# A two-block transformer kernel on one core: the gated delta-rule scan by column halves with both directions in one output product, and the second block's convolution, index choice and attention in another arrangement of PSUM banks

## The chip, the cores and the metric

The kernel runs on one core of a Trainium2 chip. The core has TensorE (PE in the rows; PEld is its weight load), VectorE (DVE), ScalarE (ACT), GpSimd (POOL) and SyncE (SP, which issues most DMAs). Each engine takes its instructions in the order in which they stand in its own queue, and semaphores hold an instruction until what it reads is written and what it overwrites is free. The metric is the device time of one execution in microseconds (us); a time is the median of several runs.

## What is computed

A model in two blocks, all in fp32, for 256 tokens ("lat") and 256 context tokens ("ctx") of 1024 features. The first block has two layers; the mixer of its layer 0 is a gated delta-rule network (GDN) scanned in both directions, beside a latent attention (MLA). The second block has two layers, each with a mixer (sparse attention, a causal convolution with 31 taps, a pooling) and a feed-forward part.

```python
# GDN: one step of the scan, for each of 8 heads, chunks of 64 tokens, state s of 64x64
v_new = u_i - einsum('bhck,bhkv->bhcv', w_i, s)
o_i = einsum('bhck,bhkv->bhcv', qd_i, s) + einsum('bhcs,bhsv->bhcv', qk_i, v_new)
s = s * gl_i[..., None, None] + einsum('bhck,bhcv->bhkv', kd_i, v_new)
# run over ctx, then lat, forwards, and over both flipped, backwards; the two outputs are added

# second block, mixer of a layer; u = rmsnorm(h) @ w_in, cut into q, k, v, qi, ki, wi, u_conv, u_pool
idx = einsum('bths,bth->bts', relu(einsum('bthd,bsd->bths', qi, ki)), wi) * idx_scale   # 16 index heads
_, sel = lax.top_k(where(causal, idx, -inf), 64)       # for each token the 64 keys that it may attend
y_attn = softmax over the chosen keys (q k) @ v        # 8 heads of 64, 2 kv heads, query blocks of 128
y_conv = silu(layernorm(conv31(a * sigmoid(g)) + conv_b)) @ conv_pw     # 256 channels
y_pool = windowed means @ pool_w * pool_scale
mix = concatenate([y_attn, y_conv, y_pool]) @ w_out
```

## The kernel before, in words

A projection in fp32 is made of three matmuls on split operands (`mm3`, L554 to L556: high by high, low by high, high by low); weights come by DMA into `wraw`, ACT casts them to `whi` (L270) and DVE or POOL makes the low half `wlo` (L272). Plain fp32 matmuls stand in the rows with two PE instructions each, transposes with one. PSUM has eight banks of 128x512 fp32, handed out by kind from `Banks`; a bank of a kind is taken again only when the readers of its last content are done. The order of the instructions in each engine's queue is made while the program is built: a planner in the framework takes the instructions of the program text and interleaves them wherever their operands and buffers allow it by its own estimate of durations. So work written one after the other (the scan, then MLA) runs interleaved, and what stands in the rows is the planner's order.

**The scan (layer 0).** The kinds are `g` 3 banks, `s` 2, `tp`, `po` and `gv` one each; `aux` is `g` and `acc` is `s`. `gdn_run` (L1216) goes over four blocks i of 128 tokens and, in each, first over direction 0 and then over direction 1 (which walks the blocks in the order 1, 0, 3, 2 and the halves of a block backwards). `gdn_operands` makes a block's operands: `pu` (L1158) and two `pw` (L1160, L1163), three banks of `g`, which ACT copies to `gu` (L1165) and `gwq` (L1168, L1169). `gdn_state` then takes the two halves `a` of 64 tokens: `ps` = w and q times the state (L1192, four 128x128 matmuls), `gvn` = u minus `ps` (DVE, L1195), `pS` = kd^T times gvn (L1199: for each of four head pairs a 64x128 by 64x128 product into 128 partitions, of which only the two 64x64 blocks on the diagonal are used), the state S times its decay (POOL, L1206) plus `pS` (DVE, L1207), and `po` = Q times gvn (L1210, eight 64x64 products, all with the same half of the rows). `gdn_o` (L1175) adds the outputs. Around that, while the scan waits, PE runs `mod_chunk` (L373, the modulation vectors) and `l0_mla` (L787): four pairs of heads with two scores and two softmaxes each in `attend` (L665: scores, L676 maximum, L678 exp, L681 transposes into the scores' own bank, L683 copy, L689 value products into `po`). The first two pairs use the two `s` banks for scores, the late ones one `s` and one `g`; the tags `p` and `pt` have K.np = 2 buffers. `gdn_post` and `gdn_out` (L1252) end the layer's mixer.

**The mixer of the second block**, run twice (`s_mixer`, L1677). The kinds are `acc` 2 banks, `aux` 1, `s` 2, `tp` 2, `po` 1. The program's text is: `choose(1)` and later `choose(0)` (index scores of query block 1 or 0 into `s`, relu on ACT L1614 into `irl`, weighting on DVE L1621, then `s_topk`: eight rounds of MAX8 and MATCH_REPLACE8 on DVE, L1636 and L1637, and the mask L1639), the projections, `qkv`, `conv` (L1540: for each of two channel halves c and 32 taps, of which the last is the bias, a product for each of two token blocks; one block in `po`, one in `tp`), `pool_out`, `finish` (batch statistics L1551, reciprocal root in small DVE steps, `lnx` L1556 which reads the convolution's banks, transposes L1559 into an `acc` bank, then L1562, L1565 and the products L1569), and `att(1)`, `att(0)`. `s_attend` is called for each of two groups and makes two units hh: scores with the mask (L1654 and mm3) into `s`, maximum L1657, exp L1662, transposes L1664 into `tp`, a copy L1665, value products L1669 into the single `po` bank, scaling L1673. `out_features` transposes the result (L728, L306). The products with `w_out` follow. The weight pool `K.px` of the projections is closed after the mixer (L2037).

## Time and profile before

| | before |
|---|---|
| median of 3 runs | 2125.01 us (2121.82 to 2138.47) |
| the profiled execution, its own time | 2124.6 us |
| its span in the profile | 2122.8 us |
| PE busy | 1991.6 us, 94% of the span |
| DVE, ACT, POOL busy | 62%, 44%, 11% |
| mean granted TensorE clock | 0.957 of full speed |

A row of a stretch gives the busy time of each engine with its number of instructions, the granted clock of TensorE (1.00 is 2.4 GHz, 0.50 is 1.2 GHz) and what the DMAs moved. In a row of the timeline several equal instructions that follow one another are put together (x8), and what stands in brackets is how long the engine sat idle before it, and for whom.

### The profile page before, as it was taken

How to read it: one execution, taken by the hardware profiler on the slowest of the kernel's cores; microseconds unless marked ns; L12 is line 12 of the kernel's file. 1: busy time of each engine (PE TensorE's matmuls, PEld its weight loads, DVE VectorE, ACT ScalarE, POOL GpSimd, SP SyncE). 2: the span in 40 equal slices, each digit the busy share in tenths (PEclk: the TensorE clock that was granted, in tenths of full speed). 3: DMA queues.
4: the chain of work that ended last, by engine and by line, in shares of the span. 5: the costliest groups of instructions: out<-in, count | busy, mean ns of one | idle time of the engine just before them, and what ended most of it. 6: DMA issues, size and time to landing. Idle time of an engine off the chain costs nothing.

```text
span 2122.8 us, 31144 instructions
## 1 busy us (share of the span) xinstructions
PE 1991.6 (94%) x11656; PEld 1626.7 (77%) x11656; DVE 1315.5 (62%) x2729; ACT 924.7 (44%) x1620; POOL 242.1 (11%) x312
## 2 busy tenths in 40 slices
PE   6989799889999999979898999998999999989998
PEld 3868468768888778868666888897788789868886
DVE  5557457766777754454786555575765558576644
ACT  4533443354222233343565443564554445555532
POOL 2120212301000000020401001110200021020000
PEclk8999789899999999989898999998999999999999
DMA  8344542132568542213235664522656535055551
GB/s 284 90 120 101 179 130 66 46 109 80 179 213 279 164 158 90 89 53 120 70 99 159 184 194 137 155 87 62 197 179 190 180 97 147 21 169 184 188 188 66
DMA packets 186951, 291.88 MB, mean 137 GB/s; under 512 B 28472, under 2 KB 75704, under 8 KB 186800
## 3 DMA queue, kind: packets, MB, share of 16 engines
q1 hardware_dynamic: 172720, 272.54, 41.2%
q0 software_dynamic: 5472, 16.13, 2.4%
q10 hardware_dynamic: 8608, 1.23, 0.5%
q8 instruction: 91, 1.49, 0.3%
q14 instruction: 60, 0.49, 0.1%
HBM read 281.44 MB, written 8.41 MB: 137 GB/s over the span
## 4 chain that ended last, share of the span: by engine, by line
PE 85%; DVE 5%; DMA 4%; ACT 3%; issue 2%; POOL 1%; SPq 0%; ACTq 0%; DVEq 0%; POOLq 0%
PE acc L554 19%; PE acc L556 19%; PE acc L555 19%; PE s L554 3%; PE s L555 2%; PE s L556 2%; PE po L689 2%; PE tp L890 2%; PE po L1540 1%; PE tp L1540 1%; DMA wraw<-in_w_mod_dram 1%; PE gv L373 1%; PE aux L728 1%; PE aux L489 1%; PE g L1199 1%
## 5 line engine op out<-in xcount | busy, mean ns | idle before, releaser
L272 DVE TENSOR_TENSOR wlo<-wraw,whi 128x512 fp32r<-128x512 f32 (+4 forms) x772 | 483.4, 670 | 299.1 <-ACT whi L270 283.3
L270 ACT CAST whi<-wraw 128x1024 fp32r<-128x1024 f32 (+4 forms) x420 | 413.5, 990 | 496.4 <-PE acc L556 192.9
L554 PE MATMUL acc<-whi,u 128*128 128x512 f32 (+3 forms) x1320 | 508.5, 388 | 15.4 <-ACT u L306 9.6
L556 PE MATMUL acc<-whi,u 128*128 128x512 f32 (+3 forms) x1320 | 505.2, 384 | 1.7 <-DVE u L307 1.7
L555 PE MATMUL acc<-wlo,u 128*128 128x512 f32 (+3 forms) x1320 | 506.0, 385 | 0.2 <-DVE wlo L272 0.2
L554 PEld LDWEIGHTS acc<-whi,u 128*128 128x128 f32 x1320 | 251.3, 191 | 66.0 <-ACT u L306 11.6
L556 PEld LDWEIGHTS acc<-whi,u 128*128 128x128 f32 x1320 | 251.0, 190 | 50.4 <-DVE u L307 3.8
L555 PEld LDWEIGHTS acc<-wlo,u 128*128 128x128 f32 x1320 | 251.4, 191 | 47.4 <-DVE wlo L272 1.4
L554 PE MATMUL acc<-u,whi 128*128 128x512 f32 (+1 forms) x480 | 171.0, 362 | 1.8 <-ACT u L306 1.7
L555 PE MATMUL acc<-u,whi 128*128 128x512 f32 (+1 forms) x480 | 171.0, 358 | 0.2 <-DVE u L307 0.2
L556 PE MATMUL acc<-u,wlo 128*128 128x512 f32 (+1 forms) x480 | 171.1, 360 | 0.0
L272 POOL TENSOR_TENSOR wlo<-wraw,whi 128x512 fp32r<-128x512 f32 (+1 forms) x68 | 84.7, 1276 | 409.7 <-ACT whi L270 409.7
L432 DVE SCALAR_TENSOR_TENSOR msum<-mraw,u,msum 128x512 f32<-128x512 f32 x140 | 100.8, 747 | 15.2 <-DMA mraw<-in_w_mod_dram 14.1
L554 PEld LDWEIGHTS acc<-u,whi 128*128 128x128 f32 x480 | 91.0, 191 | 17.4 <-issue 2.6
L555 PEld LDWEIGHTS acc<-u,whi 128*128 128x128 f32 x480 | 91.9, 192 | 15.0 <-issue 1.7
L556 PEld LDWEIGHTS acc<-u,wlo 128*128 128x128 f32 x480 | 91.5, 191 | 15.0 <-issue 1.7
L307 DVE TENSOR_TENSOR u<-aux,u 128x512 fp32r<-128x512 f32 (+2 forms) x96 | 59.5, 632 | 41.0 <-ACT u L306 40.8
L554 PE MATMUL acc<-whi,dxh 128*128 128x512 f32 x176 | 69.7, 396 | 1.9 <-ACT dxh L306 1.9
L306 ACT CAST u<-aux 128x512 fp32r<-128x512 f32 (+2 forms) x96 | 50.6, 543 | 47.6 <-PE aux L728 34.9
L555 PE MATMUL acc<-wlo,dxh 128*128 128x512 f32 x176 | 69.6, 396 | 0.0
L556 PE MATMUL acc<-whi,dxl 128*128 128x512 f32 x176 | 69.0, 396 | 0.0
L307 DVE TENSOR_TENSOR dxl<-u,dxh 128x1024 fp32r<-128x1024 f32 x22 | 26.7, 1225 | 52.5 <-ACT dxh L306 52.5
(521 smaller groups left out, 3089.6 us busy)
## 6 DMA issues: line engine op xcount, KB each, us to landing
wraw<-in_w_up_dram SPq DMA_DIRECT2D x64, 512.0 KB, 4.0
wraw<-in_w_down_dram SPq DMA_DIRECT2D x64, 512.0 KB, 4.0
mraw<-in_w_mod_dram SPq DMA_DIRECT2D x56, 512.0 KB, 4.7
wraw<-in_w_ffn_down_dram SPq DMA_DIRECT2D x44, 512.0 KB, 3.8
wraw<-in_w_mod_dram SPq DMA_DIRECT2D x40, 512.0 KB, 5.9
wraw<-in_w_ffn_gate_dram SPq DMA_DIRECT2D x48, 256.0 KB, 3.1
wraw<-in_w_ffn_up_dram SPq DMA_DIRECT2D x48, 256.0 KB, 3.6
wraw<-in_w_ffn_gate_dram SPq DMA_DIRECT2D x20, 512.0 KB, 4.5
```

The costliest lines, as they stand in the source:

```text
L270: self.K.nc.scalar.copy(hi, raw)
L272: e.tensor_tensor(lo[:, k], raw[:, k], hi.bitcast(F32)[:, k], op=ALU.subtract)
L306: (hi_eng or nc.scalar.copy)(hi, src)
L307: nc.vector.tensor_tensor(lo, src, hi.bitcast(F32), op=ALU.subtract)
L373: nc.tensor.matmul(ps[32 * j:32 * j + 32, :], K.cl[:, g + k, :], raw[:, k, :], start=(g + k < 4), stop=(g + k >= 4))
L432: nc.vector.scalar_tensor_tensor(accs[s], raw[:, k, :], c, accs[s], op0=ALU.mult, op1=ALU.add)
L554: mm(ps, ah, bh, start=start, stop=False)
L555: mm(ps, ah, bl, start=False, stop=False)
L556: mm(ps, al, bh, start=False, stop=stop)
L689: nc.tensor.matmul(po[hh * 64:hh * 64 + 64, c:c + 128], v(hh, j), pts[hh][0][:, j * 128:(j + 1) * 128], start=(j == 0), stop=(j == nj - 1))
L890: nc.tensor.matmul(tp[:, t * 128:(t + 1) * 128], x[:, t // 2, t % 2 * 128 + j:t % 2 * 128 + j + 128], dg[j], start=(j == 0), stop=(j == 4))
L1540: nc.tensor.matmul(ps[t][:, c * 128:c * 128 + 128], yp[:, c, t * 128 + j:t * 128 + j + 128] if j < 31 else ones, dg, start=(j == 0), stop= ...
```

## The change

In the scan, `gdn_state` makes `pS` of 64x64 products, eight in the place of four of 64x128, which alternate between the two column halves hh and write only what is used; it uses half a bank. The product `po` is taken out of it: `gdn_run` makes the operands of both directions first, then for each of the two steps of a block the state of direction 0 and of direction 1, and then one `po` bank for both, with the products of the two directions alternating (direction 0 and 1 use different halves of the rows and of the partitions). In MLA the units of the first two pairs rotate over `s`, `s`, `tp`, those of the late ones over `s`, `s`, `tp`, `g`, `g`, `g`, with three `p` and `pt` buffers.

In the second block the convolution has one bank for both token blocks; the bias is one 512-wide product at its beginning (from four scaled identities in `irl` buffers) in the place of the 32nd tap. `att(1)` is written ahead of `conv` and `choose(0)`, in a pool of its own, for which the weight pool of the projections is closed inside the mixer. A unit of attention uses one bank for scores and transposes (`s` for hh = 0, `tp` for hh = 1), four `p` and `pt` buffers, and its value products go to `acc`; the transposes of `finish` go to `aux`.

```diff
@@ l0_mla
+    used = [0]
+    def unit(kinds):
+        used[0] += 2
+        return [kinds[(used[0] + i) % len(kinds)] for i in range(2)]
+    K.np = 3
...
-                   ("s", "g") if late else ("s", "s"))
+                   unit(("s", "s", "tp", "g", "g", "g") if late else ("s", "s", "tp")))
@@ gdn_state
-    pS, po = aux(K), aux(K)
+        gdn_o(K, t, a, slice(64 - 64 * a, 128 - 64 * a), ps)
+    pS = aux(K)[:, :256].rearrange("p (q c) -> p q c", q=4)
     for p in range(4):
-        c = slice(p * 128, (p + 1) * 128)
-        nc.tensor.matmul(pS[:, c], kd[r, c], vn[r, c], start=True, stop=True)
+        for hh in range(2):
+            c = slice(p * 128 + hh * 64, p * 128 + hh * 64 + 64)
+            nc.tensor.matmul(pS[hh * 64:hh * 64 + 64, p, :], kd[r, c], vn[r, c], start=True, stop=True)
...
-    for h in range(8):
-        hs = slice(h * 64, h * 64 + 64)
-        nc.tensor.matmul(po[o, hs], Q[r, h, :], vn[r, hs], start=True, stop=True)
@@ gdn_run
-        for d in range(2):
-            t = i if d == 0 else (1, 0, 3, 2)[i]
-            ops = gdn_operands(K, d, t)
-            for a in ((0, 1) if d == 0 else (1, 0)):
-                gdn_state(K, d, i == 0 and a == d, t, a, *ops, K.S[d])
+        ts = [i, (1, 0, 3, 2)[i]]
+        ops = [gdn_operands(K, d, ts[d]) for d in range(2)]
+        for s in range(2):
+            vns = []
+            for d in range(2):
+                u, wq, kd, Q = ops[d]
+                a = s ^ d
+                vns.append((64 * a, Q, gdn_state(K, d, i == 0 and s == 0, ts[d], a, u, wq, kd, K.S[d])))
+            po = aux(K)
+            for h in range(8):
+                hs = slice(h * 64, h * 64 + 64)
+                for a, Q, vn in vns:
+                    K.nc.tensor.matmul(po[64 - a:128 - a, hs], Q[a:a + 64, h, :], vn[a:a + 64, hs], start=True, stop=True)
@@ s_conv
-        ps = [bank(K, "po"), bank(K, "tp")]
+        ps = bank(K, "po")
+        bias = cut(K, [128, 2, 256], F32, "irl", 3)
...
+        nc.tensor.matmul(ps, ones, bias.rearrange("p t f -> p (t f)"), start=True, stop=False)
...
-        back = acc(K)
+        back = aux(K)
@@ s_attend
-        ps = bank(K, "s")
+        ps = bank(K, ("s", "tp")[hh])
...
-        p, pt = cut(K, [128, 512], F32, "p", 2), cut(K, [128, 512], F32, "pt", 2)
-        tp = bank(K, "tp")
+        p, pt = cut(K, [128, 512], F32, "p", 4), cut(K, [128, 512], F32, "pt", 4)
+        tp = ps
...
-        po = bank(K, "po")
+        po = acc(K)
@@ s_mixer
-        cv = conv()
-        choose(0)
-        pool_out(0)
-        pool_out(1)
-        finish(cv)
-        att(1)
-        att(0)
+        closed(K, K.px)
+        W.drop()
+        with Pool(K, "at"):
+            att(1)
+            with On(K, pix):
+                cv = conv()
+                choose(0)
+                pool_out(0)
+                pool_out(1)
+                finish(cv)
+            att(0)
```

What the planner makes of it shows in the queues. The first place is PE's queue in the scan, one block after its start. Before, it reads as follows (`gwq`, `gkd`, `gQ` are the operands, `gu` and `gvn` the values u and v_new, `gv` is a modulation vector, `s` a bank of MLA):

```order
L1192 MATMUL g_2378<-u_129,gwq_2354 128x128 x4
L373 MATMUL gv_3299<-wraw_3300,u_124 32x512 x2
L373 MATMUL gv_3299<-wraw_3304,u_124 32x512 x2
L819 MATMUL s_3535<-const_id_75,u_3388 128x128 x4
L819 MATMUL s_3542<-const_id_75,u_3388 128x128 x4
L1199 MATMUL g_2385<-gvn_2383,gkd_2309 128x128 x4
L1210 MATMUL g_2386<-gvn_2383,gQ_2359 64x64 x8
```

In the changed program the same engine has at this place (L1200, L1209 and L1237 are the lines of w and q, of `pS` and of `po` now):

```order
L1209 MATMUL g_2464<-gvn_2461,gkd_2309 64x64 x8
L1200 MATMUL g_2477<-u_130,gwq_2408 128x128 x4
L373 MATMUL gv_3355<-wraw_3364,u_124 32x512 x2
L554 MATMUL s_3614<-whik_3608,u_3438 128x512
L555 MATMUL s_3614<-wlok_3609,u_3438 128x512
L556 MATMUL s_3614<-whik_3608,u_3439 128x512
L373 MATMUL gv_3355<-wraw_3368,u_124 32x512 x2
L1209 MATMUL g_2485<-gvn_2482,gkd_2363 64x64 x8
L1237 MATMUL g_2498<-gvn_2461,gQ_2359 64x64
L1237 MATMUL g_2498<-gvn_2482,gQ_2413 64x64
```

`pS` stands as eight small products, other work stands between the steps of the two directions, and `po` of both directions stands behind both states, the two taking turns. All 16 products of `po` in a step read this way. The scan's last product is row 1080 of PE's queue before and row 1190 now, and the work of MLA's later pairs stands behind it in both.

The second place is PE's queue at the end of the second block's first mixer. Before, behind the last product of the convolution and the scores of query block 0:

```order
L1559 MATMUL acc_12895<-const_id_75,lnx_12917 128x128 x2
L1669 MATMUL po_12967<-u_11625,pt_12958 128x64 x4
L1559 MATMUL acc_12895<-const_id_75,lnx_12921 128x128 x2
L1664 MATMUL tp_13049<-const_id_75,p_13047 128x128 x4
L1669 MATMUL po_12997<-u_11625,pt_12988 128x64 x4
L1664 MATMUL tp_13086<-const_id_75,p_13084 128x128 x2
L1569 MATMUL aux_12935<-u_12894,u_11638 128x256
```

Now the queue has there, with L1582 and L1592 as the lines of `finish` and L1677 as that of the mask (`u_11684`):

```order
L556 MATMUL s_13030<-u_12033,u_12105 128x128
L554 MATMUL s_13030<-u_12033,u_12111 128x128
L555 MATMUL s_13030<-u_12034,u_12111 128x128
L556 MATMUL s_13030<-u_12033,u_12112 128x128
L1582 MATMUL aux_13077<-const_id_75,lnx_13099 128x128 x2
L1582 MATMUL aux_13077<-const_id_75,lnx_13103 128x128 x2
L1592 MATMUL aux_13117<-u_13076,u_11694 128x256 x2
L1677 LDWEIGHTS u_11652
L1677 MATMUL s_13127<-u_11684,u_11652 128x128
```

The value products of query block 1 have moved ahead of the convolution's end. The last index scores of `choose(0)` (`s_13030`) have moved from the middle of the convolution to behind its last product, and all eight score products of query block 0 stand behind them and behind `finish`; between these two places PE has nothing else.

The third place is DVE's queue there. Before, the choice of query block 0 begins amid the convolution (`ply` belongs to the pooling, `u_11626` holds the index values):

```order
L1523 TENSOR_SCALAR ply_12883<-aux_12880,u_73 128x256
L1621 SCALAR_TENSOR_TENSOR u_11626<-irl_12855,u_11979,u_11626 128x128
L1621 SCALAR_TENSOR_TENSOR ipart_12770<-irl_12855,u_11979,ipart_12770 128x128
L307 TENSOR_TENSOR u_11602<-ply_12883,u_11601 128x256
L1622 TENSOR_TENSOR u_11626<-u_11626,ipart_12770 128x128
L1633 TENSOR_TENSOR u_11626<-u_11626,const_rest_11594 128x128
L1636 MAX m_12861<-u_11626 128x8
L1637 MATCH_REPLACE u_11626<-m_12861,u_11626 128x128
```

Now it begins among the small steps of the reciprocal root for the convolution's layer norm (`rsv`, `rsy`, `rst`), behind the convolution's end:

```order
L1645 TENSOR_TENSOR u_11682<-u_11682,ipart_12952 128x128
L327 SCALAR_TENSOR_TENSOR rsy_13087<-rst_13088,rsy_13087 128x2
L1656 TENSOR_TENSOR u_11682<-u_11682,const_rest_11650 128x128
L325 TENSOR_TENSOR rst_13088<-rsy_13087 128x2
L1659 MAX m_13043<-u_11682 128x8
L326 TENSOR_TENSOR rst_13088<-rst_13088,rsv_13085 128x2
L1660 MATCH_REPLACE u_11682<-m_13043,u_11682 128x128
```

Behind these rows the eight rounds go on, with `lnx`, `cz` and the end of `finish` among them, up to the mask (L1662), which the scores of query block 0 read.

## Rows read from the trace of the kernel before

**Rows 1.** The page's busy times: engine, busy us, share of the span, instructions.

```profile
PE 1991.6 (94%) x11656; PEld 1626.7 (77%) x11656; DVE 1315.5 (62%) x2729; ACT 924.7 (44%) x1620; POOL 242.1 (11%) x312
```

**Rows 2.** Stretches of the scan and mixers: busy time of each engine, clock, DMA.

```profile
core 0: us, PE busy (x) PEld busy (x) DVE busy (x) ACT busy (x) POOL busy (x), PEclk, DMA share, GB/s
266.00:320.00 54.00, 51.73 (x607) 38.39 (x607) 29.33 (x67) 23.42 (x46) 6.38 (x10) 0.90 0.42 130
355.00:425.00 70.00, 62.36 (x575) 51.61 (x573) 49.50 (x100) 22.20 (x57) 21.62 (x30) 0.83 0.13 39
1340.00:1453.00 113.00, 112.81 (x820) 104.70 (x818) 74.03 (x203) 65.10 (x157) 9.91 (x12) 1.00 0.36 101
1453.00:1474.00 21.00, 15.04 (x89) 12.97 (x89) 11.66 (x40) 7.23 (x23) 1.14 (x2) 0.78 0.04 15
1845.00:1870.00 25.00, 18.85 (x116) 15.98 (x114) 13.08 (x44) 7.33 (x23) 1.14 (x2) 0.82 0.04 13
```

**Rows 3.** Two 5 us stretches amid the second row above, the same columns.

```profile
400.00:405.00 5.00, 5.00 (x32) 4.66 (x30) 4.56 (x17) 0.00 (x0) 0.00 (x0) 0.50 0.00 0
415.00:420.00 5.00, 3.17 (x19) 2.39 (x18) 4.93 (x14) 2.13 (x6) 2.81 (x4) 1.00 0.28 89
```

**Rows 4.** Timeline of PE in the scan: start, duration, line, tile, count.

```profile
302.25 0.98 PE L1158 MATMUL g<-u,u 64*64 64x64 f32 x27
304.15 0.97 PE L1160 MATMUL g<-u,gke 64*64 64x64 f32 x32
330.12 1.16 PE L1199 MATMUL g<-gvn,gkd 64*128 64x128 f32 x8
331.20 1.14 PE L1210 MATMUL g<-gvn,gQ 64*64 64x64 f32 x16
348.68 1.09 PE L689 MATMUL po<-pt,u 128*64 128x128 f32 x14
```

**Rows 5.** Timeline near the scan's end: copies of operands, and a wait of PE.

```profile
395.89 0.59 ACT L1165 COPY gu<-g 128x512 f32<-128x512 f32 x1 [5.01 <-PE g L1158]
397.17 0.41 ACT L1169 COPY gwq<-g 128x256 f32<-128x256 f32 x1
399.69 1.79 PE L1199 MATMUL g<-gvn,gkd 64*128 64x128 f32 x8 [1.18 <-DVE gvn L1195]
```

**Rows 6.** Timeline of PE at the end of the second block's first mixer.

```profile
1448.77 0.39 PE L1540 MATMUL po<-dg,u 128*128 128x128 f32 x2
1452.54 0.27 PE L556 MATMUL s<-u,u 64*128 64x128 f32 x1
1456.17 0.69 PE L1559 MATMUL acc<-const_id,lnx 128*128 128x128 f32 x2 [3.35 <-DVE lnx L1556]
1459.53 1.81 PE L1669 MATMUL po<-u,pt 128*128 128x64 f32 x8
1463.78 1.00 PE L1669 MATMUL po<-u,pt 128*128 128x64 f32 x8
1470.59 0.66 PE L1669 MATMUL po<-u,pt 128*128 128x64 f32 x4 [0.16 <-DVE u L1673]
1473.87 0.80 PE L554 MATMUL acc<-whi,u 128*128 128x512 f32 x1 [1.62 <-ACT whi L270]
```

**Rows 7.** Timeline of that mixer: index choice, scores, maximum and exp of block 0.

```profile
1427.34 0.29 DVE L1633 TENSOR_TENSOR u<-u,const_rest 128x128 f32<-128x128 f32 x1
1436.79 0.29 DVE L1639 TENSOR_TENSOR u<-u,const_rest 128x128 bf16<-128x128 f32 x1
1445.17 0.22 PE L1654 MATMUL s<-u,u 128*128 128x128 bf16 x1
1445.80 0.23 PE L1654 MATMUL s<-u,u 128*128 128x128 bf16 x1
1450.59 0.42 DVE L1657 TENSOR_REDUCE anx<-s 128x2 f32<-128x256 f32 x1 [3.55 <-PE s L556]
1447.06 0.37 ACT L1662 ACTIVATE p<-s,anx 128x128 f32<-128x128 f32 x1 [0.53 <-DVE rs L1672]
```

More of the change, by code (lines that the diff above doesn't have):

```diff
@@ L1180, in gdn_o, with gdn_state @@
         K.nc.scalar.copy(K.O[o, t, :], ps[o])
-def gdn_state(K, d, first, t, a, u, wq, kd, Q, S):
+def gdn_state(K, d, first, t, a, u, wq, kd, S):
     nc = K.nc
     r = slice(64 * a, 64 * a + 64)
-    o = slice(64 - 64 * a, 128 - 64 * a)
     if first:
@@ L1218, in gdn_run @@
     for i in range(4):
-        for d in range(2):
-            t = i if d == 0 else (1, 0, 3, 2)[i]
-            ops = gdn_operands(K, d, t)
-            for a in ((0, 1) if d == 0 else (1, 0)):
-                gdn_state(K, d, i == 0 and a == d, t, a, *ops, K.S[d])
+        ts = [i, (1, 0, 3, 2)[i]]
[11 more added lines that the diff above has]
+                    K.nc.tensor.matmul(po[64 - a:128 - a, hs], Q[a:a + 64, h, :], vn[a:a + 64, hs], start=True, stop=True)
+            for d in range(2):
+                a = s ^ d
+                gdn_o(K, ts[d], a, slice(64 - 64 * a, 128 - 64 * a), po)
 def gdn_post(K):
@@ L1526, in taps @@
     def taps(c):
-        for j in range(32):
+        for j in range(31):
             if j % 3 == 0:
                 dg = cut(K, [128, 3, 128], F32, "dg", 2)
-            nc.scalar.mul(dg[:, j % 3, :], K.ident, dw[:, i, c, j:j + 1] if j < 31 else dwb[:, i, c:c + 1])
+            nc.scalar.mul(dg[:, j % 3, :], K.ident, dw[:, i, c, j:j + 1])
             yield j, dg[:, j % 3, :]
     def conv():
-        ps = [bank(K, "po"), bank(K, "tp")]
+        ps = bank(K, "po")
+        bias = cut(K, [128, 2, 256], F32, "irl", 3)
+        for t in range(2):
+            for c in range(2):
+                nc.scalar.mul(bias[:, t, c * 128:c * 128 + 128], K.ident, dwb[:, i, c:c + 1])
+        nc.tensor.matmul(ps, ones, bias.rearrange("p t f -> p (t f)"), start=True, stop=False)
         for c in range(2):
@@ L1539, in conv @@
                 for t in range(2):
-                    nc.tensor.matmul(ps[t][:, c * 128:c * 128 + 128],
-                                     yp[:, c, t * 128 + j:t * 128 + j + 128] if j < 31 else ones, dg,
-                                     start=(j == 0), stop=(j == 31))
-        return ps
+                    nc.tensor.matmul(ps[:, t * 256 + c * 128:t * 256 + c * 128 + 128],
+                                     yp[:, c, t * 128 + j:t * 128 + j + 128], dg,
+                                     start=False, stop=(c == 1 and j == 30 and t == 1))
+        return [ps[:, t * 256:t * 256 + 256] for t in range(2)]
     def finish(ps):
         y = cut(K, [128, 2, 256])
-        back = acc(K)
+        back = aux(K)
         mv = cut(K, [128, 2, 2], F32, "bmv", 1)
@@ L1714, in qkv @@
             pairs_T(K, U[:, t, 0:512], 4, qh, ql, tk, 0.125)
-    with Pool(K, "ix"):
+    with Pool(K, "ix") as pix:
         choose = s_index(K, U, idx, mask)
```

12 lines of the change are left out of this document (4 added, 8 removed).

## The prediction, made before the changed kernel had run

> **What bounds the kernel now.** I read the page's busy times first: PE is busy for 94% of the span [rows 1], so a gain must take work from PE, fill one of the few stretches in which it waits or runs at the lower clock, or lengthen none. Then the table of stretches [rows 2]. Work at full clock is busy time times granted clock. From 355 to 425 us, the end of the scan with MLA beside it, 62.36 us of busy time at 0.83 are 51.8 us of work in 70 us: 18.2 us are lost. From 266 to 320 us it is 46.6 of 54 us, 7.4 lost. The second block's mixer is full until its convolution ends (112.81 of 113 us at 1.00), and then has a tail: 1453 to 1474 us holds 15.04 busy us at 0.78, 11.7 us of work in 21. The second run of the mixer has the same tail (18.85 busy of 25 us at 0.82). The two stretches of 5 us [rows 3] show the two forms of loss in the scan: all busy at 0.50 (2.5 us lost), or 3.17 busy at 1.00 (1.8 lost). At 399.69 PE waits 1.18 us for `gvn` with nothing else in its queue [rows 5]. Whatever the change does elsewhere, these two places decide.
>
> **The scan's products.** `po`: before, 16 steps of 16 instructions, 1.14 us each [rows 4], all in one quadrant of the array. A pair of directions takes 2.28 us, about 2.1 as the second overlaps the first one's end. Now the 32 instructions of a pair alternate between two quadrants that share neither rows nor columns. The nearest rows are L1158, 27 such instructions in 0.98 us, alternating so into one bank, and L1160, 32 in 0.97 us into two. I take 1.05 us; saved 1.05, in 8 pairs 8.4 us.
>
> The trace so far says that two row halves may write one bank at full pace: L1158 does [rows 4]. The Trainium skill's page "TensorEngine Tiling (Array Packing)", section Restrictions and Gotchas, says that different row tiles cannot access the same PSUM bank simultaneously; by that rule the pair would take turns and save nothing, and the sum below would come out 8.4 us higher. Here the row decides; the case is a rival below.
>
> `pS`: before, 8 instructions, and the next line starts 1.08 us later (330.12 to 331.20) [rows 4]. Now 16 of half the columns, alternating between column halves over the same rows. L689 alternates column halves with 128 columns: 14 instructions in 1.09 us, 0.06 apart, where L1199's are 0.13 apart. With 64 columns and the same overlap they would be 0.03 apart: 0.5 us. Without overlap the pace is that of L1210's 64x64, 0.06 apart: 1.0 us. I take 0.55 as L1158 has the same shape and 0.03; saved 0.53, in 16 steps 8.5 us (bounds 1.3 and 9.3). Together PE's work falls by 17 us; from 1 us if no halves overlap.
>
> **The scan's waits.** Products of MLA and of the modulation now stand between the two directions' steps, and the scan ends at a row of PE's queue with MLA's first pairs still unfinished, so the waits for `gvn` are covered to the end. MLA's late pairs then run on six banks instead of two. Of the 18.2 us lost I give back 12; the rest stays, because a softmax's chain of maximum, exp, transposes and copy still has to run for the last units. Bounds 5 and 18. On the other side, operands of direction 1 stand directly behind those of direction 0 and need the same three `g` banks, which ACT copies out one after the other, 395.89 to 397.58, 1.7 us [rows 5]. In four blocks that is 7 us at most, 0 where other products cover; I take 4. `gQ` is loaded for both directions at once, but is read only in the last product of a step; later loads on SP's queue don't stand behind a wait that is longer than before. Scan: -17 - 12 + 4 = -25 us.
>
> **The second block's tail.** Edits that I cost at nothing: the convolution has 124 products and one four times as wide instead of 128, each 0.39 us or less [rows 6]; ACT makes 66 scaled identities instead of 64, ahead of PE as now. Both lie in the full stretch; uncovered, the bias would cost its own product and two of the four extra identities, under 3 us. The earlier closing of the weight pool lets nothing start sooner that PE waits for: the first product with `w_out` waits for ACT's cast behind the last split of the attention [rows 6], and still does.
>
> What moves is dearer. Ahead of the convolution's end come four value products of block 1, 1.00 us each [rows 6], and eight transposes for them, by the 0.69 us of two at half clock about 1.4 us: +5.4. Behind it go six units of scores of block 0, 0.63 us each (1445.17 to 1445.80) [rows 7]: -3.8. So the last index scores end at about 1452.8 + 1.6 = 1454.4 us (1452.8 is the end of the last score before the wait, rows 6). Then the choice of block 0, which lay under the convolution, is exposed, because its eight rounds on DVE start only now and the scores of block 0 wait for its mask. Before, it took from 1427.34 to 1437.08, 9.7 us, with seven foreign instructions in between [rows 7]. Now some sixteen foreign ones stand between, small ones mostly, for which I add 1.0, and 1.2 for the relu and the weighting of the last unit ahead of it: 11.9 us in which PE has only `finish`, about 1.5 us of work. Then eight units of scores. PE came back to full clock some 6 us after it resumed at 1456.17: eight instructions of L1669 took 1.81 us at 1459.53 and 1.00 at 1463.78 [rows 6]. The units are 5.0 us of work, and 6 us at half clock lose 3: 8.1. Behind the last score come maximum (0.42), two exps (0.37 each and their sums) [rows 7], transposes and a copy, together 2.2, and from the last value products to `w_out` 1470.59 to 1473.87 [rows 6], 3.3. So `w_out` would start at 1454.4 + 11.9 + 8.1 + 5.5 = 1479.9 us instead of 1473.87: 6.0 later, in two mixers +12 us. Bounds for one mixer: -1, if the choice needs 8 us and the clock stays, and +9, if the foreign instructions hold each round up.
>
> **Sum.** 2124.6 us for the profiled execution (its span is 2122.8, the rest lies around it), -25 and +12: 2111.6. The median of the runs is 0.4 us higher than that execution, so I say 2112.
>
> **Rivals.** *A, the forecast:* own range 2102 to 2122, chance 0.52.
>
> *B, the scan becomes dense and the tail costs little:* -17 and all of the 18.2 us, tail +2 in all: 2092. It speaks for it that MLA's rest now lies behind the scan with six banks; against it that the last units of MLA have nothing behind them and that PE's clock follows each gap. Chance 0.22. Half-way cases give 2094 to 2103.
>
> *C, the change doesn't do what it says in the scan:* the products get shorter, but the steps are bound by the way over DVE and POOL, so shorter products only make the waits longer, as the 1.18 us wait at 399.69 suggests [rows 5]. Then the gain is 9 us and the tail takes 12: 2128. Against it: before 355 us PE hardly waits. Chance 0.11.
>
> *D, the other side:* operands. If each of four double blocks stops PE for 4 us (two rounds of copies with no product that can pass) and half clock follows for 6 us (3 us), 28 us are lost; with -17 and +12 that is 2148. It decides from 5 us in each block on, where the kernel gets slower at all with nothing recovered. Against it: the queue has other products around three of the four blocks. Chance 0.10.
>
> *E, row halves wait for each other in `po`'s bank:* 8.4 us of the saving go: 2120. Chance 0.05, as L1158's pace [rows 4] speaks against it. This is the rule of the skill's page that stands above.
>
> **How the numbers follow.** About 1%, 21 us, is what a measurement of this kernel can tell from no change: faster is below 2104, slower above 2146. Faster: B and the lower end of A, 0.27. Slower: most of D and a little of C, 0.10. Between: 0.63. The range goes from B's middle, 2096, to just above C, 2131; outside lie D with 0.10 and the lower half of B with 0.10.
>
> **What would show it.** Right, if the products of `po` stand in the new profile as 32 in about 1 us and 16 of `pS` in about 0.5; if the scan's last stretch shows little idle time for `gvn`; and if in both mixers of the second block PE idles some 10 us between the last index scores and the mask, at half clock behind it, with `w_out` about 6 us later than the convolution's end would have it now. Wrong, if PE waits for ACT's copies at the operands (D), if 16 of `pS` still take 1 us, or if the rounds of the choice run ahead of the convolution's end.

## The result, and the profile of the changed kernel

The changed kernel takes 2105.9 us (median of 4 runs, 2103.1 to 2107.4) where the kernel before took 2123.9 beside it. The ratio is 0.9899 with a 95% interval of 0.9854 to 0.9945: by the ratio 21 us less, with an interval of 12 to 31; the two medians lie 18 us apart. Forecast were 2112 us, in a range of 2096 to 2131, and most of the chance within 1%; the ratio lies on that line. The direction is right and the gain of 13 us was taken some 5 to 8 us too small. The profiled execution of the changed kernel took 2107.4 us, the longest of the four; its span is 2105.6 us. One execution of a later run, of 9858 us with MLA's banks alone, counts in no time and no ratio below.

The page of the changed kernel, its span and the busy times:

```profile
span 2105.6 us, 31388 instructions
PE 1966.8 (93%) x11772; PEld 1603.0 (76%) x11772; DVE 1309.4 (62%) x2729; ACT 927.2 (44%) x1626; POOL 241.8 (11%) x312
```

PE has 25 us less busy time than before [rows 1] and the span is 17 us shorter. The table of stretches shows the two places that decided: the scan (two rows, the same stretches as in [rows 2]) and the tail of the second block's first mixer (three rows; the mixer lies 33 us earlier now).

```profile
core 0: us, PE busy (x) PEld busy (x) DVE busy (x) ACT busy (x) POOL busy (x), PEclk, DMA share, GB/s
266.00:320.00 54.00, 49.70 (x763) 36.42 (x758) 37.21 (x77) 24.62 (x55) 11.83 (x16) 1.00 0.48 151
355.00:425.00 70.00, 61.24 (x515) 46.46 (x513) 62.67 (x125) 34.98 (x86) 17.64 (x26) 0.97 0.18 61
1420.00:1424.00 4.00, 0.62 (x3) 0.46 (x4) 3.98 (x23) 0.00 (x0) 0.00 (x0) 0.60 0.56 173
1424.00:1429.00 5.00, 2.57 (x7) 1.30 (x6) 4.75 (x21) 1.22 (x3) 0.00 (x0) 0.50 0.21 76
1433.00:1440.00 7.00, 7.00 (x24) 4.95 (x23) 1.61 (x5) 2.34 (x10) 0.00 (x0) 0.50 0.00 0
```

In the scan the clock is 1.00 from 266 to 320 us where it was 0.90, and 0.97 from 355 to 425 where it was 0.83 [rows 2]. The second pair of rows doesn't hold the same work: the last product of `po` starts at 373.2 us now and started at 410.1 before. In the tail PE is busy for 0.62 of 4 us and then, from 1433 to 1440, for all of 7 us at 0.50. The timeline of PE in the scan (start, duration, line, tile, count) shows the new products:

```profile
330.53 0.68 PE L1209 MATMUL g<-gvn,gkd 64*64 64x64 f32 x16
331.14 1.16 PE L1200 MATMUL g<-u,gwq 128*128 128x128 f32 x8
335.31 1.09 PE L1237 MATMUL g<-gvn,gQ 64*64 64x64 f32 x29
336.34 1.16 PE L1200 MATMUL g<-u,gwq 128*128 128x128 f32 x8
```

Sixteen instructions of `pS` take 0.61 us up to the next line, and `po` of both directions stands as one run of 29 in 1.09 us, whose first three are mixed with the end of `pS` just before: these rows answer [rows 4]. The timeline of the mixer's tail, PE and DVE:

```profile
1418.50 0.27 PE L556 MATMUL s<-u,u 64*128 64x128 f32 x1
1423.38 1.14 PE L1582 MATMUL aux<-const_id,lnx 128*128 128x128 f32 x4 [4.62 <-DVE lnx L1579]
1428.71 0.29 DVE L1662 TENSOR_TENSOR u<-u,const_rest 128x128 bf16<-128x128 f32 x1
1429.06 0.29 PE L1677 MATMUL s<-u,u 128*128 128x128 bf16 x1 [0.73 <-DVE u L1662]
1430.11 0.29 PE L1677 MATMUL s<-u,u 128*128 128x128 bf16 x1
1434.32 2.07 PE L1592 MATMUL aux<-u,u 128*128 128x256 f32 x4
1436.19 0.31 PE L1677 MATMUL s<-u,u 128*128 128x128 bf16 x1
1447.93 0.79 PE L554 MATMUL acc<-whi,u 128*128 128x512 f32 x1 [1.62 <-ACT whi L270]
```

The last index score ends at 1418.8 us, the mask (L1662) at 1429.0, the first score of query block 0 stands at 1429.06, and the first product with `w_out` at 1447.93. Between the index score and the mask PE waited 4.62 us for `lnx`. A score product with its mask takes 1.05 us here (1429.06 to 1430.11), 0.63 before [rows 7]. The second output product of `finish` (L1592, 1434.32) stands among the scores, and not ahead of all eight of them as the section on the change has it. [Rows 6] had 1452.8 for the end of the last score ahead of the wait, one of query block 0, and 1473.87 for `w_out`.

To set stretches of two executions side by side I use a line that both have and that stands ahead of each stage, the scaled transposes L489: its first row opens the feed-forward part behind the scan, the first of `ndg,xn` the second block's first mixer. Kernel before and changed kernel:

```profile
L489 PE MATMUL aux<-ndg,u x160: 270/275/580, 494.5 to 1136.9; 128*128 128x128 f32 x160
L489 PE MATMUL aux<-ndg,xn x64: 270/275/553, 1325.5 to 1731.7; 128*128 128x128 f32 x64
```

```profile
L489 PE MATMUL aux<-ndg,u x160: 270/275/582, 459.9 to 1103.6; 128*128 128x128 f32 x160
L489 PE MATMUL aux<-ndg,xn x64: 270/275/551, 1292.9 to 1707.6; 128*128 128x128 f32 x64
```

By these rows the changed kernel is 34.6 us ahead behind the scan, 32.6 at the first mixer, and 17.2 at the end. From the mixer's first product to the first product with `w_out` it takes 155.0 us (1292.9 to 1447.93) where it took 148.4 (1325.5 to 1473.87). The second block's second mixer reads alike: PE waits 4.62 us for `lnx` once more, and the same stretch takes 149.7 us (1702.75 to 1852.46) where it took 142.9 (1726.87 to 1869.78).

### The profile page after: what moved, and what is told of

It reads as the page before. It is cut to its first block, busy times and chain, and to the rows that moved or that the text cites. A ratio compares the mean times of both kernels' runs of the same rounds, so it can differ in the third digit from the quotient of the medians.

```text
span 2105.6 us, 31388 instructions
## 1 busy us (share of the span) xinstructions
PE 1966.8 (93%) x11772; PEld 1603.0 (76%) x11772; DVE 1309.4 (62%) x2729; ACT 927.2 (44%) x1626; POOL 241.8 (11%) x312
## 4 chain that ended last, share of the span: by engine, by line
PE 80%; DVE 8%; DMA 6%; ACT 3%; issue 2%; POOL 1%; SPq 0%; ACTq 0%; DVEq 0%; POOLq 0%
PE acc L554 18%; PE acc L556 18%; PE acc L555 18%; PE po L1563 3%; PE s L554 2%; PE s L555 2%; PE s L556 2%; PE tp L898 2%; PE po L689 1%; DMA mraw<-in_w_mod_dram 1%; PE gv L373 1%; DVE wlo L272 1%; DMA wraw<-in_w_mod_dram 1%; PE aux L728 1%; ACT whi L270 1%
## 5 line engine op out<-in xcount | busy, mean ns | idle before, releaser
L1563 PE MATMUL po<-dg,u 128*128 128x128 f32 x496 | 62.3, 278 | 0.0
```

The lines of the kernel that those rows point to most:

```text
L1563: nc.tensor.matmul(ps[:, t * 256 + c * 128:t * 256 + c * 128 + 128], yp[:, c, t * 128 + j:t * 128 + j + 128], dg, start=False, stop=(c == ...
```

## The experiments

All times below are medians; a ratio is to the kernel before on the same chip, where it ran at 2126.4, 2126.4 and 2122.9 us. The theory is the prediction's: the scan brings about 25 us, by shorter products and by waits that are covered, and each mixer of the second block loses about 6 because the choice of block 0 is exposed and TensorE's clock falls behind it. The first expectations take larger sizes for the two, 33 and 8 us, from the profiles of the result.

### The scan with MLA's banks, without the second block

The second block's functions are as before; the rest of the diff stands.

> The scan's steps and MLA's banks as in the changed kernel, the second block as before. Theory: in the changed kernel the scan brings some 33 us (the first transposed product of the feed-forward part stands at 459.9 us instead of 494.5) and the second block costs some 8 us in each of its two mixers, so without the second block's edits the time is 2105.9 - 15 = about 2091 us. Rival: the second block's loss is only the planner's shift of work that would be paid elsewhere anyway, and the scan alone gives about 2106 us.

Measured: 2101.5 us, ratio 0.9886 (0.9844 to 0.9929), 24 us less than before. The four times reach from 2094.4, the profiled one, to 2103.3. This is 10 us above the theory's number and 4 below the rival's. The profile's rows:

```profile
L489 PE MATMUL aux<-ndg,u x160: 270/275/580, 460.3 to 1106.4; 128*128 128x128 f32 x160
L489 PE MATMUL aux<-ndg,xn x64: 270/275/551, 1295.0 to 1701.2; 128*128 128x128 f32 x64
```

The scan is over at 460.3 us as in the changed kernel (459.9), and from there to the end of the span (2092.6) it takes 1632.3 us, against 1645.7 in the changed kernel: 13.4 us is what the second block's edits cost in this pair of executions, of which one was the shortest of its kernel and the other the longest. The medians show 4 us and the ratios 3, on different chips and with intervals that overlap, so the timed runs of this pair don't show the loss; the second block alone, below, does. The scan's gain by timed runs is 24 us.

### The steps of the scan alone, and MLA's banks alone

```diff
# steps alone: gdn_state and gdn_run as changed, l0_mla as before
# MLA alone:   l0_mla as changed, gdn_state and gdn_run as before
```

> Only the scan's steps are changed (products by column halves, both directions in one output product); MLA keeps its banks and two buffers, the second block is as before. Theory: the shorter products (17 us) and the directions' steps with other work between them carry most of the gain, so 2124 - 25 = about 2099 us, with MLA's late pairs some 8 us slower than with the new banks. Rival: the clock and the waits come back only because MLA's late pairs have six banks, so the steps alone bring 12 us or less: about 2112 us or above.

> Only MLA's banks and buffers are changed (units rotate over s, s, tp and over six banks in the late pairs, three p and pt buffers); scan and second block are as before. Theory: the steps of the scan bring nearly all of the gain, MLA's banks alone 5 us or less: about 2121 us. Rival: the waits near the scan's end in the kernel before were MLA's waits for its two score banks; then the banks alone bring 12 us or more: 2114 us or less.

Measured: the steps alone 2104.2 us, ratio 0.9908 (0.9881 to 0.9934), 20 us less; MLA's banks alone 2120.8 us, ratio 0.9999 (0.9978 to 1.0021), no difference. The first is 5 us above its theory and 8 below the rival, the second fits its theory. The stretch from 355 to 425 us, first with the steps, then with MLA's banks:

```profile
core 0: us, PE busy (x) PEld busy (x) DVE busy (x) ACT busy (x) POOL busy (x), PEclk, DMA share, GB/s
355.00:425.00 70.00, 60.03 (x460) 43.69 (x459) 57.50 (x114) 28.16 (x72) 16.46 (x23) 0.98 0.20 61
```

```profile
355.00:425.00 70.00, 61.36 (x569) 50.20 (x570) 46.87 (x94) 21.25 (x53) 22.52 (x31) 0.82 0.14 43
```

With the steps the clock is 0.98, with the banks 0.82, as before (0.83 [rows 2]), though with the steps the last `po` starts at 370.6 us and what follows in the stretch is other work. By the timed runs the gain is that of the steps; what PE lost near the scan's end was not a lack of banks for MLA. Banks and steps together are 0.0022 better than the steps alone, with intervals that overlap; whether the banks bring anything is not settled.

### The scan's two products, each undone in the changed kernel

```diff
# po: one direction after the other, in the same bank
-            for h in range(8):
-                hs = slice(h * 64, h * 64 + 64)
-                for a, Q, vn in vns:
+            for a, Q, vn in vns:
+                for h in range(8):
+                    hs = slice(h * 64, h * 64 + 64)
# pS: four products of 128 columns, as before
+        c = slice(p * 128, (p + 1) * 128)
+        nc.tensor.matmul(pSb[:, c], kd[r, c], vn[r, c], start=True, stop=True)
```

> The changed kernel with the two directions of the scan's output product one after the other (eight of direction 0, then eight of direction 1, in the same bank) instead of alternating. Theory: without the alternation the 32 instructions of a pair take about 2.1 us instead of 1.1, and TensorE's work in the scan grows by 8 us; most of it is on the path: about 2112 us. Rival (row halves cannot write one bank together, or the scan is bound by the way over VectorE): the same products take as long as alternating, or the longer ones fill waits, and the time stays within 3 us of 2106.

> The changed kernel with pS as before: four products of 128 columns into a whole bank instead of eight by halves. Theory: 16 steps cost 1.08 us instead of 0.62, 7 us more work on TensorE, on the path: about 2112 us. Rival: the state's chain over POOL and VectorE bounds the steps and pS only fills a wait: within 3 us of 2106.

Measured: `po` apart 2115.2 us, ratio 0.9948 (0.9929 to 0.9967); `pS` wide 2111.7, ratio 0.9940 (0.9904 to 0.9975). Against the changed kernel's ratio that is 10 and 9 us, the first with intervals that overlap at their edges (0.9929 to 0.9945), the second with intervals that overlap widely. In the profiles the part behind the scan begins at 465.7 us with `po` apart and at 464.4 with `pS` wide; in the eight profiles with the changed scan and banks it begins between 459.8 and 463.9. Both point to a cost, smaller in these profiles than by the timed runs, and its size is not settled. The timeline of PE at the same step, with `po` apart:

```profile
336.76 1.67 PE L1237 MATMUL g<-gvn,gQ 64*64 64x64 f32 x29
338.36 1.16 PE L1200 MATMUL g<-u,gwq 128*128 128x128 f32 x8
```

and with `pS` wide, where `po` alternates without `pS` in between (the row of L1208 is `pS`):

```profile
334.76 1.16 PE L1208 MATMUL g<-gvn,gkd 64*128 64x128 f32 x8
335.85 1.15 PE L1237 MATMUL g<-gvn,gQ 64*64 64x64 f32 x32
336.93 1.16 PE L1200 MATMUL g<-u,gwq 128*128 128x128 f32 x8
```

Apart, 29 instructions take 1.67 us; alternating, 32 take 1.15 and the next line starts 1.08 us after the first. They write the same bank, each direction its own half of the partitions, so two row halves do write one bank at the faster pace, which settles rival E against it. The Trainium skill's sentence in "TensorEngine Tiling (Array Packing)", Restrictions and Gotchas, that different row tiles cannot access the same PSUM bank simultaneously, does not hold in these rows: by it both orders would take equally long. `pS` wide starts 1.09 us before its follower (334.76 to 335.85), by halves 0.61.

### The second block alone

First block as before, second block as changed.

> Only the second block is changed (convolution in one bank, attention ahead of it, closing of the weight pool), the first block is as before. Theory: the choice of query block 0 is exposed behind the convolution and TensorE runs at half clock after it: +8 us in each mixer, so about 2139 us. Rival: the tail's loss comes from what the scan's change moved (loads, buffers), and alone the second block is within 3 us of before, about 2124 us.

Measured: 2132.7 us, ratio 1.0035 (1.0013 to 1.0057), 7 us slower than before (3 to 12). The theory had 2139 us, the rival about 2124; the time lies between. The tail is the changed kernel's. Its two rows on PE, the wait for `lnx` and the first product with `w_out`, and the rows of L489:

```profile
1449.80 1.14 PE L1565 MATMUL aux<-const_id,lnx 128*128 128x128 f32 x4 [4.62 <-DVE lnx L1562]
1474.34 0.79 PE L554 MATMUL acc<-whi,u 128*128 128x512 f32 x1 [1.62 <-ACT whi L270]
```

```profile
L489 PE MATMUL aux<-ndg,u x160: 270/275/579, 486.6 to 1131.5; 128*128 128x128 f32 x160
L489 PE MATMUL aux<-ndg,xn x64: 270/275/553, 1320.3 to 1731.5; 128*128 128x128 f32 x64
```

From the mixer's first product to `w_out` it takes 154.0 us (1320.3 to 1474.34), as in the changed kernel and 5.6 more than before; the second mixer takes 149.9 us (1726.61 to 1876.49), 7.0 more. So the loss is the second block's own, and the rival falls. The first of the rows of L489 tells something else too: with the scan untouched, and PE's work up to there in the same order in both traces, the part behind it begins at 486.6 us here and at 494.5 in the profile of the kernel before. So the same scan can differ by 8 us between two executions, and by this yardstick only 27 of the 34.6 us between the first two profiles belong to the change. It bears on this run as well: its span is 8.4 us longer than before, with 12.6 more in the two mixers and 7.9 less ahead of L489. Whether the timed 7 us hold such a gain in the scan is open.

### What the tail is made of: work in the idle time

```diff
+        if t == 0:                                  # end of choose(0)
+            warm = acc(K)
+            for _ in range(20):
+                nc.tensor.matmul(warm[:, :256], K.ident, rl[:, :, :n], start=True, stop=True)
# second run, moreover, in s_attend behind each score product of block 0
+            for _ in range(6 if t == 0 else 0):
+                nc.tensor.matmul(ps[:, 256 + x * 128:384 + x * 128], K.identb, mask[:, :n], start=True, stop=True)
```

> The changed kernel with 20 more products (identity by the last relu values, 256 columns, into a free acc bank, read by nobody) behind the last index scores of choose(0) in each mixer of the second block, so that TensorE works while VectorE makes the choice. Theory: the loss behind the mask is the lower clock after the idle time; with the clock kept at 1.00 the scores take 5 us instead of 11 and the rest of the tail shortens too, about 8 us in each mixer: about 2090 us. Rival: the clock falls because the scores are small products over half of the rows, not because of the idle time; then the scores still run at 0.50 and the time is 2106 us or a little above.

> As the run with 20 idle-time products, and behind each score product of query block 0 six more products over all 128 rows (identity by mask, read by nobody, into unused columns of the same bank). In the run before the clock fell to 0.50 some 4 us into these scores though TensorE was never idle. Theory: it fell because the score products use half of the rows; with full-row products in between the clock stays at 1.00 through the scores, and the time is about 2102 us in spite of 3 us more work in each mixer. Rival: it falls at the same distance behind the wide products whatever runs there, and the time is 2108 us or more.

Measured: with the 20 products 2102.5 us, ratio 0.9886 (0.9851 to 0.9921); with full-row products among the scores too 2104.1 us, ratio 0.9911 (0.9880 to 0.9943). Neither can be told from the changed kernel by its time; the theory of the first had 2090. The tables of stretches behind the mask tell more. First the run with the 20 products, whose scores begin at 1428.3:

```profile
core 0: us, PE busy (x) PEld busy (x) DVE busy (x) ACT busy (x) POOL busy (x), PEclk, DMA share, GB/s
1428.00:1432.00 4.00, 4.00 (x28) 3.15 (x26) 2.58 (x7) 2.26 (x10) 0.00 (x0) 0.99 0.44 131
1432.00:1436.00 4.00, 4.00 (x15) 3.13 (x15) 1.16 (x5) 1.81 (x11) 0.00 (x0) 0.50 0.00 0
```

then the run with full-row products among the scores, the same stretches:

```profile
1428.00:1432.00 4.00, 4.00 (x43) 3.34 (x42) 2.35 (x6) 1.64 (x6) 0.00 (x0) 1.00 0.39 131
1432.00:1436.00 4.00, 4.00 (x35) 3.08 (x35) 1.44 (x4) 1.90 (x8) 0.00 (x0) 1.00 0.00 0
```

The scores that ran at 0.50 in the changed kernel start at 0.99 when PE was kept at work: the idle time was the cause there. But in the first run the clock falls to 0.50 by 1432 us, with PE busy for 4.00 of 4 us on either side. In the second it stays at 1.00. The programs differ only in the added products over all 128 rows between score products that use 64. So the first expectation's two readings were each partly right: the clock was low behind an idle stretch, and it also fell in a run of scores without any idle time. That the half of the rows is what made it fall is not shown: the added products differ from the scores in type and number too. From the mixer's first product to `w_out` the first run takes 151.3 us, the second 152.5, where the changed kernel took 155.0. So the idle time costs some 4 us of this stretch, and in the second run the time of the added products outweighs what the higher clock gives back.

### Where the choice and the convolution are called

Three runs keep all of the changed kernel and move calls inside the second block.

```diff
# A: choose(0) first, then att(1), conv, pool_out, finish, att(0)
# B: conv, choose(0), att(1), pool_out, finish, att(0)
# C: as A, and
-        bias = cut(K, [128, 2, 256], F32, "irl", 3)
+        bias = cut(K, [128, 2, 256], F32, "cbias", 1)
-            po = aux(K)                         # products of finish
+            po = both[:, d * 256:d * 256 + 256]     # both = bank(K, "po")
```

A:

> The changed kernel with one call moved: choose(0) ahead of att(1) and of the convolution. Theory: with the mask of query block 0 ready under the convolution, scores and value products of both blocks fit under it and only finish stands behind it; the stretch from the convolution's end to the first product with w_out falls from 29 us to about 18, in two mixers 22 us: about 2084 us. Rival: the choice's scores and its DVE rounds only push the attention of block 1 back, and the tail keeps most of its length: about 2100 us.

B:

> The changed kernel with the calls of the second block in the order convolution, choose(0), att(1), pooling and finish, att(0); banks and buffers as changed. Theory: choose(0) runs under the convolution again without standing alone before it, attention of both blocks fills TensorE up to finish, and from the mixer's first product to the first product with w_out it takes about 145 us instead of 155 (149 before): about 2086 us. Rival: with the convolution over early nothing covers the chain of the last softmaxes, and the stretch is as long as before, 149 us: about 2094 us.

C:

> As the run with choose(0) called first, with two edits: the four scaled identities of the convolution's bias have a buffer of their own instead of the relu's three, and both output products of finish go to the convolution's bank, which is free by then. Theory: that run lost 5 us in each mixer because the convolution could not start under choose(0), its bias waiting for the relu's buffers, and 3 us because the products of finish took turns on one bank; without both, from the mixer's first product to the first with w_out it takes 148 us instead of 156, and the time is about 2099 us. Rival: the loss is the clock and not the wait, and the time stays above 2108 us.

Measured: A 2114.6 us, ratio 0.9950 (0.9929 to 0.9972); B 2099.1, ratio 0.9868 (0.9839 to 0.9897); C 2098.0, ratio 0.9883 (0.9853 to 0.9913). A was a miss by 30 us, and by its median worse than the changed kernel (the intervals overlap at their edges). The timeline of PE shows where it lost, with the tail's end in the third row, and the stretch around the loss under it:

```profile
1385.99 0.69 PE L1366 MATMUL aux<-const_id,akd 128*128 128x128 f32 x2 [0.67 <-DVE u L653]
1387.98 2.05 PE L1559 MATMUL po<-irl,u 128*128 128x512 f32 x2 [1.29 <-ACT irl L1558]
1454.64 0.79 PE L554 MATMUL acc<-whi,u 128*128 128x512 f32 x1 [1.62 <-ACT whi L270]
```

```profile
core 0: us, PE busy (x) PEld busy (x) DVE busy (x) ACT busy (x) POOL busy (x), PEclk, DMA share, GB/s
1382.00:1394.00 12.00, 10.00 (x44) 8.00 (x43) 11.52 (x49) 4.43 (x13) 0.00 (x0) 0.57 0.25 85
```

The choice alone, whose scores wait for relu buffers and they for DVE, leaves PE idle in pieces, and the convolution can't fill them: its bias needs the same buffers (`irl`) and waits for ACT. Twelve us pass with 10.00 busy at 0.57; over the whole stretch to `w_out` A's first mixer takes 1.2 us more than the changed kernel's and its second 7.2 (156.9). The tail did shrink as the theory said, from 29 us to 15 (1439.6 to 1454.64). C takes the shared buffer away and gets 148.7 us from the first product to `w_out` where A took 156.2; it came out at the theory's number. It holds a second edit, the bank for the products of `finish`, and what each of the two brought is not told apart. B gets 149.8 us, not 145: the rival's stretch, and a time 5 us above the rival's. A row of its scores and its last stretch show two causes:

```profile
1424.75 1.10 PE L1692 MATMUL acc<-u,pt 128*128 128x64 f32 x8
```

```profile
core 0: us, PE busy (x) PEld busy (x) DVE busy (x) ACT busy (x) POOL busy (x), PEclk, DMA share, GB/s
1424.00:1426.00 2.00, 2.00 (x16) 1.68 (x16) 1.18 (x8) 1.49 (x8) 0.00 (x0) 1.00 0.00 0
1426.00:1430.00 4.00, 4.00 (x22) 3.64 (x22) 2.00 (x12) 1.85 (x9) 0.00 (x0) 0.60 0.00 0
1430.00:1435.00 5.00, 5.00 (x21) 3.02 (x21) 3.80 (x14) 0.61 (x2) 0.43 (x1) 0.50 0.00 0
```

PE is busy throughout and the clock falls to 0.50 all the same: the convolution's products are over by 1423.1 us, and what is left are score products of block 0 and other small ones. That is the fall of the run with the 20 products once more; but here eight instructions of value products over all 128 rows (1424.75) stand among the scores, and the clock falls nevertheless. The other cause is the rival's: behind 1435 us only `finish` and the transposes of its result are left, and PE is busy for 6.4 of the 11.4 us from 1435.64 to `w_out` (1447.08).

### Only the value products in another bank

Scan and MLA as changed; of the second block two lines.

```diff
-        po = bank(K, "po")          # s_attend
+        po = acc(K)
-        back = acc(K)               # finish
+        back = aux(K)
```

> Scan and MLA as changed; of the second block only two edits: the value products go to an acc bank instead of the single po bank, and the transposes of finish to aux; the order of calls, the convolution in two banks and all else are as before. Theory: the tail before was a wait for the po bank, which the convolution holds until lnx; without it the value products of block 1 run under the convolution and the scores of block 0 cover finish, so the stretch from the mixer's first product to the first with w_out falls from 149 to about 143 us, in two mixers 11 us below the run with the scan alone (2101.5): about 2091 us. Rival: the softmax chain and the lower clock take the place of the wait and the time stays at 2101 us.

Measured: 2085.9 us, ratio 0.9827 (0.9795 to 0.9859), the fastest of all, 37 us below the kernel before; by the ratios 12 below the scan alone and 15 below the changed kernel, with intervals that overlap at their edges in both pairs. The theory had 2091. PE's timeline at the end of its first mixer:

```profile
1424.48 1.11 PE L1686 MATMUL acc<-u,pt 128*128 128x64 f32 x8
1432.64 1.06 PE L1576 MATMUL aux<-const_id,lnx 128*128 128x128 f32 x4
```

Value products of block 1 now stand in the convolution and right behind it, and `finish` (L1576) follows among other products without a wait, where the kernel before waited 3.35 us for `lnx` [rows 6]. The profiled execution took 2092.7 us, the others 2082.8 to 2087.2, and shows a granted clock of 0.95 in stretches where other profiles show 1.00, so its stretches are no measure of the gain: its mixers take 147.3 and 141.0 us from the first product to `w_out`, where the scan alone took 148.8 and 142.8 and the theory had 143 for the first. That the wait is gone is shown; that it makes up the whole 12 us is not.

## Why the prediction held, and where its terms were off

**Scan, -25.** Measured 24 us by the run with the scan alone (interval 15 to 33), 27 by the profiles with the run of the second block alone as the yardstick. The size was right.

**Its products, -17.** `pS` 0.61 us instead of 1.08: 16 times 0.47 is 7.5, forecast 8.5. `po` from about 2.1 us to 1.03 to 1.25 (335.09, its first instruction, to 336.34 in the changed kernel; 1.08 with `pS` wide): 7 to 8.5, forecast 8.4. By the timed runs the undone products cost 10 and 9 us, with wide intervals. This term holds, and with it the reading of L1158, L1210 and L689 as the nearest rows. One point was off: in the same bank, but not alternating, the pair takes 1.83 us (336.53 to 338.36), not 2.1, so the alternation itself saves about 0.6 to 0.75 us a pair, 5 to 6 in eight, and the rest goes with having both directions in one run.

**Its waits, -12 + 4.** The stretches that the forecast named hold other work now, so I take the whole stage instead, from 266 us to the first row of L489: the kernel before, the run of the second block alone (the scan as before), and the changed kernel, in the columns of the tables above.

```profile
266.00:494.50 228.50, 211.96 (x1913) 166.55 (x1913) 151.47 (x305) 92.86 (x207) 40.17 (x54) 0.92 0.27 86
266.00:486.60 220.60, 200.97 (x1752) 157.12 (x1753) 148.43 (x286) 88.60 (x201) 40.62 (x54) 0.95 0.27 84
266.00:459.90 193.90, 178.07 (x1917) 137.74 (x1913) 146.48 (x297) 89.26 (x204) 40.73 (x54) 0.97 0.30 98
```

Busy time times clock, good to some 2 us as the clock has two digits, is 195, 191 and 173 us of work; lost are 33.5, 29.7 and 21.2. So the work fell by 18 to 22 us, forecast 17, and 8 to 12 us of lost time came back, where the two sub-terms together forecast 8. The mechanism was another than the one forecast: PE sits idle for 16.5, 19.6 and 15.8 us, hardly less, and what shrank is the loss to the lower clock, from 17 and 10 us to 5. The waits for `gvn` between 266 and 425 us were not covered to the end: 2.3 us before, 1.6 now. Why the clock stays higher in the new order is not tested. I had also given part of the gain to MLA's banks; alone they bring nothing.

**Second block, +12.** The place was right, and that the choice is exposed there: the mask comes 10.2 us behind the last index scores (forecast 11.9), and `w_out` stands 6.6 us later behind the mixer's first product (155.0 instead of 148.4) and 6.8 in the second mixer, forecast 6.0 each. Inside a mixer the terms were off and nearly cancelled. The last product ahead of the wait ends 125.9 us behind the first product where it ended 127.3 before, 1.4 earlier and not 1.6 later. From the first score to the end of the last it took 11.2 us (1429.06 to 1440.2) instead of 8.1. The step "PE came back to full clock some 6 us after it resumed" failed, as PE stayed at 0.50 until the first products with `w_out`, but this explains little of the difference: eight units at half clock are 8.4 us, by 1.05 each. The rest is the second output product of `finish`, 1.9 us, which the forecast had ahead of the mask, and 0.6 of transposes. From the last score to `w_out` it took 7.7 us instead of 5.5, at half clock too. I had read the return of the clock from a tail in which value products over all rows came first [rows 6], and here scores over half of them did; the run with full-row products among the scores kept its clock, but which property of them decides is open. Two mixers by profile cost 13 us, by the timed run with the second block alone 7 (3 to 12); the forecast of 12 lies at the edge of that, and which of the two is nearer is not settled.

**The rivals.** B, the dense scan, did not come: 21 us are still lost in the stage. C, that shorter products only lengthen waits, would leave 9 us; the scan alone brings 24 (15 to 33). D, the operands: from 266 to 425 us PE waits at the operands twice, 1.0 us for `gu` and 0.7 for `gke`, not 4 in each block. Its breaking point was reckoned wrong: with -17 and +12 the kernel gets slower from 5 us in all on, not from 5 in each block. E falls by the rows of `po`.

**The sum.** -24 and +7 by the timed runs give -17, the direct ratio -21 (12 to 31); forecast -13. By the timed runs the gap lies in the second block's term, and it is within the measurement. That the sum came so near is in part luck, as the errors inside the second block's term cancelled and the clock brought in the scan what covered waits were to bring; a ratio on the line of 1% is what the chances of 0.63 and 0.27 on its two sides leave open.

## What to carry to other kernels

Where small matmuls use one quadrant of the array, look for a second set with other rows and other columns and let the two alternate; the pace of a row that already alternates in the same trace gave the price of a pair, 1.05 us, to within 0.2. Before a call is moved ahead of a long filler, see what the last thing behind the filler will then be: here the choice of a block, a chain on another engine, came to stand where nothing was left to cover it, and a change of two lines that only freed the bank in question (value products in `acc`) did better by some 15 us than the whole rearrangement, with intervals that overlap at their edges. A buffer shared between a filler and what it should fill, as the relu's buffers and the bias, ties the two in order.

## What the runs showed of the hardware that was not expected

TensorE's granted clock fell from 0.99 to 0.50 while PE was busy without a gap (1428 to 1436 us, 4.00 of 4 us busy in both stretches) in a run of score products over 64 rows, and stayed at 1.00 in the same place when products over 128 rows stood between them. One profile of each was taken. The run with the convolution ahead shows the same fall, from 1.00 to 0.50 by 1430 us, with eight instructions of value products over 128 rows among its scores, so what decides is open. And two programs with the same scan, one of them the kernel before, reached the work behind it at 486.6 us in one execution and at 494.5 in the other, with granted clocks of 0.88 and 0.83 from 355 to 425 us: a pair of profiles can overstate the scan's gain by 8 us.
